# A third place for S5 tiles that come back from DRAM, and index gathers that stand behind the memory attention

## The chip, the core and the metric

The kernel runs on one core of a Trainium2 chip. The time is that of the device for one execution, in microseconds (us); of several executions the median is given. The profile is one execution, taken by the hardware profiler. The engines are called PE (matrix multiplication), PEld (its weight loads, which run beside it), DVE (VectorE), ACT (ScalarE), POOL (GpSimd) and SP (SyncE, which here only issues transfers).

## What is computed

One inference step of a small decoder with two layers, for a prompt of 1024 tokens and for 8 samples of 8 tokens that share the weights. Layer 0 mixes with a diagonal state-space model (S5), gates its output (GLU), and adds an attention over 256 memory tokens; layer 1 attends to a shared K/V cache with "forget" weights. This is the part that the change is about, cut from the reference:

```
# layer 0
z     = rmsnorm(h) @ w_in                              # 768 columns for S5, 256 for the memory queries
y_mem = softmax(q_mem k_mem^T / 8) v_mem               # 4 heads of 64, 256 memory tokens
y     = S5(z)                                          # scan over 48 groups of 64 states
g     = gelu(y);  y_main = g * sigmoid(g @ w_glu + b_glu)
h     = h + concat(y_main, y_mem) @ w_out              # then the MLP
# layer 1, samples only: the cached part of the forget sums
logf_past = cache_logf[page_table]                     # 8 samples x 2048 rows x 12 heads
f_past    = cumsum(logf_past)                          # used as a bias on the attention scores
```

## The kernel before, in words

Activations lie transposed: 1088 columns (1024 prompt tokens, 64 sample tokens) in four chunks `CH` of 272, features on the partitions. Every matrix product is made of three matmuls on rounded halves (`mm3`: high x high, high x low, low x high), so each operand is first split into a high and a low half: `split` has ACT write the high half (L221) and DVE, or POOL where it is told to, the low one (L222). A scheduler sets the order of instructions on each engine when the kernel is built; `after(x)` tells it that what is issued inside comes behind instruction `x`. Engines run their own rows strictly in that order, and wait for each other where data or a place in memory asks for it.

The stage around the change is called "glu". It does the following.

- The six weight tiles of `w_glu` are loaded and split; the second halves of three of them on POOL.
- The S5 output, six tiles of 128 features for all columns, had been written to DRAM (`yscr`) and is read back, re-arranged, into places `zs` of `zring` (L1280). Each tile is split into all four chunks of `yx`.
- For each of the four chunks, six output tiles `m` of the GLU: 18 matmuls each, tanh on ACT (L1324), two operations on DVE (L1325, L1326).
- After each of these 24 steps the generator `mem_attn` moves on by one unit. A unit is 128 prompt tokens and two heads: three matmuls 128x512 for the scores, a maximum (L791, DVE), two exponentials (L795, ACT), reciprocals (L796), two scalings (L798: the first on DVE, the second on POOL), four transposes on PE (L801), a copy out of PSUM (L803 ACT or L805 DVE), eight matmuls 64x128 in all for the output of a pair, and a store to `ymscr` for every second unit (L814). There are sixteen units. From the third block of tokens on, the attention of the samples moves on with them; its K and V tiles go through eight places `kvr`, cut from `extra`.
- `past_rows` (L1290 on): one index computation on POOL (L1291) and sixteen gathers, issued by POOL (L1293), that fetch cached log-forget rows by page into `fp`, which is `wf[2:4]`. `past_sums` (L1297 on): two scans on DVE over them (L1299), a copy (L1301), two subtractions (L1303), two stores to `fpast` (L1304). The sums are read only in layer 1.
- `out_proj` (L325 on) multiplies by `w_out`. Its eight raw weight tiles go through the places `wf` in turn; tiles 2 and 3, and 6 and 7, use the two places that `fp` uses. All of its loads are issued by SP, as are the stores to `fpast`.

`past_rows` is issued in the program before chunk 2, `past_sums` before chunk 3.

```
    zring = ga.sub(0, 2176).ring(2, 1088)
    extra = ga.words(4096)
```

`sub` names a part of `ga` and takes nothing from it, `words` takes; so `zring` and `extra` lie over each other, and a place of `kvr` that overlaps a place of `zring` can be loaded only when the S5 tile there has been split.

Of the kernel before, what the change touches and what calls it, by code (L numbers as in the profile page):

```python
# [12 lines left out]
ALU = mybir.AluOpType  # L13
# [35 lines left out]
def yoco_step(ctx: ExitStack, tc: tile.TileContext, I, O, upto=99, dbg=None):  # L49
    nc = tc.nc  # L50
    V, S, G, PE, SY = nc.vector, nc.scalar, nc.gpsimd, nc.tensor, nc.sync
# [251 lines left out]
    def after(ins):  # L303
        return tc.issue_after(ins.ins) if ins else nullcontext()
# [381 lines left out]
    def make_ev_qmem(l, first, ring):  # L686
# [3 lines left out]
            SY.dma_start(out=qmscr[l][:, i - first, CH[c][0]:CH[c][0] + w], in_=t)  # L690
        return ev

    def mem_attn(l, pf, pr, mb, oring, ys_to=None, extra=None):

        kb0, qr0, qf0, pw0 = pr.words(2048), pr.words(1024), pf.words(512), pf.words(3072)
# [84 lines left out]
        for b in range(8):  # L780
            qf = qfr([128, 2, 128])
            SY.dma_start(out=qf, in_=qmscr[l][:, :, 128 * b:128 * b + 128])
            qh = [qr([128, 2, 128], F32R) for _ in range(2)]
            split(qh[0], qh[1], qf)
            o = oring([128, 2, 128])
            for a in range(2):
                ps = mb([128, 2, 256])
                mm3(ps.rearrange("p e m -> p (e m)"), qh[0][:, a], qh[1][:, a], kb[0][:, a], kb[1][:, a],
                    True, True)
                st = stats([128, 12])  # L790
                V.tensor_reduce(st[:, 0:2], ps, axis=AX.X, op=ALU.max, negate=True)  # L791
                pw = prr([128, 2, 4, 128])
                p = pw[:, 0].rearrange("p (e t) m -> p e (t m)", e=2)
                for e in range(2):
                    S.activation(p[:, e], ps[:, e], AF.Exp, bias=st[:, e:e + 1], accum_out=st[:, 2 + e:3 + e])  # L795
                V.reciprocal(st[:, 4:6], st[:, 2:4])  # L796
                for e in range(2):
                    (G if e else V).tensor_scalar(p[:, e], p[:, e], st[:, 4 + e:5 + e], 0.0, op0=ALU.mult, op1=ALU.add)  # L798
                tp = mb([128, 4, 128])
                for i in range(4):  # L800
                    PE.transpose(tp[:, i, :], pw[:, 0, i, :], ident)  # L801
                if a:
                    S.activation(pw[:, 1], tp, AF.Copy)  # L803
                else:
                    V.tensor_copy(pw[:, 1], tp)  # L805
                po = mb([128, 128])
                for m in range(2):
                    for e in range(2):
                        h = 2 * a + e
                        mm(po[64 * e:64 * e + 64, :], vt[:, m, 64 * h:64 * h + 64], pw[:, 1, 2 * e + m, :],  # L810
                           m == 0, m == 1)
                S.activation(o[:, a, :], po, AF.Copy)
                if a:
                    SY.dma_start(out=ymscr[l][:, :, 128 * b:128 * b + 128], in_=o)  # L814
                if extra and b > 1:
                    next(sm, None)
                yield
# [442 lines left out]
    V.tensor_scalar(bgl, bgl, 0.5, None, op0=ALU.mult)  # L1260
    pf, pr = phase("glu", 4096, 2048 + 1024 + 1536)
    ga = joined(setA)
    zring = ga.sub(0, 2176).ring(2, 1088)
    extra = ga.words(4096)
    raws = ga.words(6 * 768)
    gring = Ring([raws.sub(384 * i, 384) for i in range(12)])
    wr_ = joined(wr)
    gwp = [wr_.sub(768 * i, 768) for i in range(10)] + [pr.words(768) for _ in range(2)]
    yx = [pair(c) for c in range(NC)]
    gw, gi = [], None  # L1270
    for i in range(6):
        raw = raws.sub(768 * i, 768).at([128, 6, 128])
        SY.dma_start(out=raw, in_=I["w_glu"][i])
        H, L = (gwp[2 * i + j].at([128, 6, 128], F32R) for j in range(2))
        x = split(H, L, raw, (G, V)[i % 2])
        gi = x if i % 2 == 0 else gi
        gw.append((H, L))
    for q in range(6):
        zs = zring([128, 8, 136])
# [26 lines left out]
    mem = mem_attn(0, pf, pr, Banks([2, 3, 4, 5, 6]), rsr, yx[NC - 1], extra)  # L1306
    for c, (t0, w) in enumerate(CH):
        if c == 2:
            with after(gi):
                past_rows()  # L1310
        if c == 3:
            with after(vi):
                past_sums()
        xH, xL = yx[c]
        held = []
        for m in range(6):
            ps = dbank([128, 512])
            for k in range(6):
                mm3(ps[:, :w], gw[m][0][:, k, :], gw[m][1][:, k, :], xH[:, k, :], xL[:, k, :],
                    k == 0, k == 5)  # L1320
            t = nt([128, w])
            y = gring([128, w])

            S.activation(t, ps[:, :w], AF.Tanh, scale=0.5, bias=bgl[:, m:m + 1])  # L1324
            V.tensor_tensor(y, xH[:, m, :].bitcast(F32), xL[:, m, :].bitcast(F32), op=ALU.add)  # L1325
            vi = V.scalar_tensor_tensor(y, t, 1.0, y, op0=ALU.add, op1=ALU.mult)  # L1326
            held.append(y)
            next(mem, None)
        n = 34 if c < NC - 1 else 26
        for m in range(6):  # L1330
            src = held[m].rearrange("p (t j) -> p t j", t=8)
            yH, yL = xH[:, m, :], xL[:, m, :]
            split(yH[:, 0:8 * n].rearrange("p (j t) -> p t j", t=8),
                  yL[:, 0:8 * n].rearrange("p (j t) -> p t j", t=8), src[:, :, 0:n], half=True)
            if c == NC - 1:
                split(yH[:, SAM].rearrange("p (t n) -> p t n", t=8),
                      yL[:, SAM].rearrange("p (t n) -> p t n", t=8), src[:, :, 26:34], half=True)
# [603 lines left out]
```

## Time and profile before

| | us |
|---|---|
| median of three runs | 2726.58 |
| the runs | 2719.97, 2726.58, 2727.91 |
| profiled execution, its own time | 2729.51 |
| its span, first to last instruction | 2727.7 |
| PE busy | 2564.0 (94 % of the span) |
| DVE busy | 1959.2 (72 %) |
| ACT busy | 1256.6 (46 %) |
| POOL busy | 1213.1 (44 %) |

"Busy" counts an engine's own operations; waiting, and issuing a transfer from SP, does not count. A start time is counted from the first instruction. A row with "x16" has put sixteen operations together; a bracket such as [5.46 <-POOL glu L798] says that the engine stood idle for 5.46 us before the row and that line 798 on POOL released it. A profile shows one execution, whose time lies a little over the median.

### The profile page before, as it was taken

To read this page: it belongs to the slowest core of one execution; us is meant where nothing else is said; L and a number is where in the kernel's file an instruction comes from. 1 tells how busy PE (TensorE), PEld (TensorE's weight loads), DVE (VectorE), ACT (ScalarE), POOL (GpSimd) and SP (SyncE) were. 2 spreads that over 40 slices of the span, in tenths; PEclk is the share of its full clock that TensorE was granted. 3 is DMA by queue.
4 is the path that set the end of the run, shared out by engine and by line. 5 is a ranking of instruction groups with operands and counts; after the bars stand their busy time and mean duration, and the time that the engine had idled before them with its cause. 6 is when DMAs were issued, how large, how long until landed. Compare 5 with 4: busy or idle time off the path is not lost.

```text
span 2727.7 us, 54053 instructions
## 1 busy us (share of the span) xinstructions
PE 2564.0 (94%) x20369; PEld 2392.2 (88%) x20369; DVE 1959.2 (72%) x3406; ACT 1256.6 (46%) x2612; POOL 1213.1 (44%) x1119
## 2 busy tenths in 40 slices
PE   6888899999998999999999999999989999899998
PEld 5777779899998999999889867777989999899998
DVE  8898665988886777794323278886588788677776
ACT  5433444566663222244322367775366665322224
POOL 4576310323321799842310455651032222179984
PEclk8999899999999999999999999999999999999999
DMA  6445352266558567443476889986226656866741
GB/s 200 106 104 146 117 163 76 91 242 243 229 228 324 232 254 277 178 167 102 150 259 222 268 290 308 304 294 218 91 87 244 236 227 234 318 242 244 285 169 67
DMA packets 242283, 561.66 MB, mean 206 GB/s; under 512 B 54053, under 2 KB 129382, under 8 KB 224614
## 3 DMA queue, kind: packets, MB, share of 16 engines
q1 hardware_dynamic: 212646, 548.50, 56.7%
q10 hardware_dynamic: 28864, 8.92, 1.4%
q8 instruction: 161, 2.64, 0.4%
q0 software_dynamic: 512, 0.79, 0.1%
q14 instruction: 100, 0.82, 0.1%
HBM read 386.19 MB, written 171.93 MB: 205 GB/s over the span
## 4 chain that ended last, share of the span: by engine, by line
PE 41%; DVE 18%; POOL 10%; DMA 10%; issue 6%; ACT 4%; SPq 0%; POOLq 0%; ACTq 0%; DVEq 0%
PE banks L209 39%; DMA hops<-plain 5%; DVE rounded L222 5%; POOL plain L630 4%; DVE plain L222 4%; PE banks L1667 1%; POOL plain L416 1%; DMA rounded<-hmid 1%; DVE plain L578 1%; POOL plain L646 1%; ACT plain L221 1%; POOL plain L422 1%; DMA hcnv<-plain 1%; POOL plain L417 1%; DMA plain<-fpast 1%
## 5 line engine op out<-in xcount | busy, mean ns | idle before, releaser
L209 PE MATMUL banks<-rounded 128*128 128x272 f32 (+3 forms) x11168 | 1552.6, 295 | 72.8 <-ACT rounded L221 18.3
L209 PEld LDWEIGHTS banks<-rounded 128*128 128x128 f32 x11168 | 1456.7, 191 | 120.3 <-ACT rounded L221 21.1
L221 ACT ACTIVATE rounded<-plain 128x512 fp32r<-128x512 f32 (+5 forms) x573 | 379.8, 676 | 637.5 <-PE banks L209 449.3
L222 DVE TENSOR_TENSOR rounded<-plain,rounded 128x512 fp32r<-128x512 f32 (+4 forms) x518 | 502.8, 976 | 121.7 <-ACT rounded L221 120.3
L209 PE MATMUL banks<-mlp,rounded 128*128 128x272 f32 x3816 | 516.8, 290 | 12.2 <-DVE plain L627 4.8
L209 PEld LDWEIGHTS banks<-mlp,rounded 128*128 128x128 f32 x3816 | 493.8, 189 | 17.2 <-DVE plain L627 5.3
L416 POOL TENSOR_TENSOR plain<-plain 128x512 f32<-128x512 f32 x60 | 103.9, 1731 | 705.9 <-DVE rounded L222 705.9
L630 POOL TENSOR_TENSOR plain<-plain,flex 128x544 f32<-128x544 f32 x192 | 289.8, 1520 | 37.7 <-DVE plain L629 34.8
L222 DVE TENSOR_TENSOR plain<-plain 128x544 fp32r<-128x544 f32 x212 | 171.1, 820 | 69.9 <-ACT plain L221 69.1
L221 ACT ACTIVATE plain<-plain 128x544 fp32r<-128x544 f32 x212 | 136.7, 650 | 111.6 <-DMA hops<-plain 99.1
L629 DVE TENSOR_TENSOR plain<-banks,plain 128x544 f32<-128x544 f32 x192 | 137.9, 718 | 50.3 <-PE banks L209 46.8
L422 POOL TENSOR_TENSOR plain<-plain 128x512 f32<-128x512 f32 x60 | 98.3, 1639 | 63.0 <-DVE rounded L222 62.6
L209 PE MATMUL banks<-flexr,rounded 128*128 128x272 f32 x816 | 114.5, 290 | 4.0 <-DVE flexr L222 4.0
L209 PE MATMUL banks<-layer 128*32 128x256 f32 (+3 forms) x1152 | 111.9, 368 | 5.5 <-DVE layer L1770 1.7
L579 ACT ACTIVATE plain<-plain 128x544 f32<-128x544 f32 (+1 forms) x136 | 83.2, 613 | 66.0 <-DVE plain L578 65.5
L209 PEld LDWEIGHTS banks<-flexr,rounded 128*128 128x128 f32 x816 | 107.8, 191 | 4.4 <-DVE flexr L222 4.4
L222 POOL TENSOR_TENSOR rounded<-plain,rounded 64x512 fp32r<-64x512 f32 (+2 forms) x55 | 77.9, 1424 | 67.1 <-ACT rounded L221 61.9
L222 POOL TENSOR_TENSOR rounded<-flex,rounded 128x544 fp32r<-128x544 f32 (+7 forms) x100 | 65.9, 668 | 83.7 <-ACT rounded L221 71.0
L578 DVE TENSOR_TENSOR plain<-banks,plain 128x544 f32<-128x544 f32 (+1 forms) x136 | 90.5, 666 | 11.8 <-PE banks L209 11.2
L222 DVE TENSOR_TENSOR rounded<-banks,rounded 128x512 fp32r<-128x512 f32 (+2 forms) x136 | 86.0, 637 | 13.1 <-ACT rounded L221 11.3
L221 ACT ACTIVATE rounded<-banks 128x512 fp32r<-128x512 f32 (+2 forms) x136 | 75.1, 559 | 42.0 <-PE banks L1667 29.3
L418 POOL TENSOR_TENSOR plain<-plain 128x512 f32<-128x512 f32 x60 | 91.7, 1528 | 2.8
(365 smaller groups left out, 3227.0 us busy)
## 6 DMA issues: line engine op xcount, KB each, us to landing
hops<-plain SPq DMA_DIRECT2D x196, 544.0 KB
rounded<-hops SPq DMA_DIRECT2D x66, 1088.0 KB
plain<-in_cache_kT SPq DMA_DIRECT2D x128, 384.0 KB
layer<-in_cache_v SPq DMA_DIRECT2D x128, 384.0 KB
mlp<-hops SPq DMA_DIRECT2D x32, 1088.0 KB
plain<-in_w_up SPq DMA_DIRECT2D x32, 1024.0 KB
plain<-in_w_down SPq DMA_DIRECT2D x28, 1024.0 KB
plain<-in_xT SPq DMA_DIRECT2D x8, 1088.0 KB
```

What stands on the lines that cost most here:

```text
L209: PE.matmul(out, a, b, start=first, stop=last)
L221: S.activation(H, src, AF.Copy)
L222: return e.tensor_tensor(L, src, H.bitcast(F32), op=ALU.subtract)
L416: G.tensor_tensor(a22, a21, a22, op=ALU.add)
L417: G.tensor_tensor(a21, a11, a21, op=ALU.subtract)
L418: G.tensor_tensor(a11, a22, a11, op=ALU.subtract)
L422: G.tensor_tensor(a12, a12, a11, op=ALU.subtract)
L578: V.tensor_tensor(x, ps, u, op=ALU.add)
L579: S.activation(x, x, AF.Relu)
L629: V.tensor_tensor(h, ps, h, op=ALU.add)
L630: G.tensor_tensor(h, h, u, op=ALU.add)
L646: G.tensor_tensor(hc, hc, hr[:, m, :], op=ALU.add)
```

## The change

Two edits. `zring` becomes three places of 1088 words instead of two; with it, places 0 to 6 of the eight `kvr` places overlap it, 0 to 4 before. And `past_rows` is ordered behind another instruction: not the third POOL split of `w_glu` (`gi`), but the last scaling of the memory attention that has been issued at that point of the program, the twelfth on POOL. No instruction is added or removed; line numbers after it are 2 or 3 higher.

```diff
+    pool = []
...
                 for e in range(2):
-                    (G if e else V).tensor_scalar(p[:, e], p[:, e], st[:, 4 + e:5 + e], 0.0, op0=ALU.mult, op1=ALU.add)
+                    pool[:] = [(G if e else V).tensor_scalar(p[:, e], p[:, e], st[:, 4 + e:5 + e], 0.0,
+                                                             op0=ALU.mult, op1=ALU.add)]
...
-    zring = ga.sub(0, 2176).ring(2, 1088)
+    zring = ga.sub(0, 3264).ring(3, 1088)
     extra = ga.words(4096)
...
-    gw, gi = [], None
+    gw = []
...
-        x = split(H, L, raw, (G, V)[i % 2])
-        gi = x if i % 2 == 0 else gi
+        split(H, L, raw, (G, V)[i % 2])
...
         if c == 2:
-            with after(gi):
+            with after(pool[0]):
                 past_rows()
```

The order of instructions is set when the kernel is built, and the two kernels' orders can be laid side by side. In the rows below a name such as glu_2469 or plain is a piece of on-chip memory, and xN counts rows that are alike.

POOL, from the three splits of `w_glu` to the sixteen scalings of the memory attention (L798), before:

```order
L222 TENSOR_TENSOR rounded<-plain,rounded 128x768 x3
L1291 TENSOR_SCALAR plain<-plain 96x16
L1293 DMA plain<-in_logf_rows,plain 96x128 x5
L703 MEMSET glu_2470 128x2048
L721 MEMSET glu_2469 128x512
L1293 DMA plain<-in_logf_rows,plain 96x128 x11
L726 COPY glu_2469<-plain 64x8x8 x4
L798 TENSOR_SCALAR glu_2469<-glu_2469,plain 128x256 x16
```

The same stretch of POOL after (L798 is now L800, L1293 is L1295):

```order
L222 TENSOR_TENSOR rounded<-plain,rounded 128x768 x3
L705 MEMSET glu_2470 128x2048
L723 MEMSET glu_2469 128x512
L728 COPY glu_2469<-plain 64x8x8 x4
L800 TENSOR_SCALAR glu_2469<-glu_2469,plain 128x256 x12
L1293 TENSOR_SCALAR plain<-plain 96x16
L1295 DMA plain<-in_logf_rows,plain 96x128 x16
L800 TENSOR_SCALAR glu_2469<-glu_2469,plain 128x256 x4
```

The index computation and all sixteen gathers moved behind twelve scalings; four scalings stand behind them.

PE at the end of the memory attention, from behind the transposes (L801) of the twelfth unit on; rows "rounded" of 272 columns are matmuls of the output projection, "glu" ones those of the attention; before:

```order
L209 MATMUL banks<-glu_2470 128x512 x3
L209 MATMUL banks<-glu_2469 64x128 x4
L209 MATMUL banks<-glu_2470 128x512 x3
L801 MATMUL banks<-plain,glu_2469 128x128 x8
L209 MATMUL banks<-glu_2469 64x128 x4
L209 MATMUL banks<-glu_2470 128x512 x3
L209 MATMUL banks<-glu_2469 64x128 x4
L209 MATMUL banks<-glu_2470 128x512 x3
L209 MATMUL banks<-rounded 128x272 x18
L801 MATMUL banks<-plain,glu_2469 128x128 x8
L209 MATMUL banks<-glu_2469 64x128 x8
L209 MATMUL banks<-rounded 128x272 x126
```

After, from the transposes of the thirteenth and fourteenth unit (the first row) on:

```order
L804 MATMUL banks<-plain,glu_2469 128x128 x8
L209 MATMUL banks<-glu_2469 64x128 x4
L209 MATMUL banks<-glu_2470 128x512 x3
L209 MATMUL banks<-glu_2469 64x128 x4
L209 MATMUL banks<-glu_2470 128x512 x3
L209 MATMUL banks<-rounded 128x272 x18
L804 MATMUL banks<-plain,glu_2469 128x128 x8
L209 MATMUL banks<-rounded 128x272 x2
L209 MATMUL banks<-glu_2469 64x128 x4
L209 MATMUL banks<-rounded 128x272 x23
L209 MATMUL banks<-glu_2469 64x128 x4
L209 MATMUL banks<-rounded 128x272 x149
```

In both, the row that follows is `rounded,mlp` x4, the first of the MLP. Ahead of the fifteenth and sixteenth unit's transposes nothing changed here; behind them 174 projection matmuls stand where 126 stood, and the third of them is the first that reads the second half of `w_out` tile 2. Projection matmuls that stood between earlier units are now behind.

DVE, around the two scans over the gathered rows (L1299) before:

```order
L805 COPY glu_2469<-banks 128x512
L1326 SCALAR_TENSOR_TENSOR plain<-flex_69,plain 128x272
L219 SCALAR_TENSOR_TENSOR rounded<-plain,rounded 128x8x34 x5
L1326 SCALAR_TENSOR_TENSOR plain<-flex_69,plain 128x272
L1299 SCALAR_TENSOR_TENSOR plain<-plain 96x1024
L219 SCALAR_TENSOR_TENSOR rounded<-plain,rounded 128x8x34
L1299 SCALAR_TENSOR_TENSOR plain<-plain 96x1024
L754 COPY glu_2469<-banks 128x256
L791 TENSOR_REDUCE plain<-banks 128x2
L1301 COPY plain<-plain 96x1
```

After (L1299 is L1301, L1301 is L1303, L1303 is L1305, L798 is L800, L805 is L808):

```order
L793 TENSOR_REDUCE plain<-banks 128x2 x2
L798 RECIPROCAL plain<-plain 128x2
L800 TENSOR_SCALAR glu_2469<-glu_2469,plain 128x256
L798 RECIPROCAL plain<-plain 128x2
L800 TENSOR_SCALAR glu_2469<-glu_2469,plain 128x256
L1301 SCALAR_TENSOR_TENSOR plain<-plain 96x1024 x2
L808 COPY glu_2469<-banks 128x512
L1303 COPY plain<-plain 96x1
L1305 TENSOR_SCALAR plain<-plain 96x1024 x2
L793 TENSOR_REDUCE plain<-banks 128x2
```

The scans moved from the middle of the GLU to between the thirteenth and fourteenth unit's scalings and the copy of their transposes. On SP the stores to `fpast` moved with them, and the loads of `w_out` tiles 2, 3, 6 and 7 now stand behind these stores; tiles 4 and 5 are loaded earlier. Before, all six stood behind the stores.

## Rows read from the trace of the kernel before

**Rows 1.** Windows: length, busy PE, PEld, DVE, ACT, POOL, granted PE clock, DMA

```profile
315.00:355.00 40.00, 40.00 (x324) 36.07 (x322) 30.82 (x60) 23.34 (x59) 3.50 (x5) 0.96 0.25 73
410.00:500.00 90.00, 89.18 (x704) 88.50 (x702) 59.21 (x83) 37.33 (x61) 6.24 (x4) 1.00 0.21 76
```

**Rows 2.** Chain of waits: start, duration, engine or transfer, line

```profile
373.06 9.60 DMA plain<-in_xT
...
386.64 2.18 DMA ymscr<-flex
388.88 3.13 DMA flex<-ymscr
...
408.54 11.53 PE banks L209 x93
```

**Rows 3.** POOL's timeline: start, duration, line, operation, idle before and releaser

```profile
283.63 0.73 POOL L1291 TENSOR_SCALAR plain<-plain 96x16 int32<-96x16 int32 x1 [11.88 <-DMA plain<-in_head_rows]
...
291.04 1.83 POOL L703 MEMSET glu<- 128x2048 f32 x1
...
293.50 0.93 POOL L1293 DMA_INDIRECT plain<-in_logf_rows,plain  x1 [0.16 <-issue]
...
297.31 2.47 POOL L1293 DMA_INDIRECT plain<-in_logf_rows,plain  x1 [0.30 <-issue]
300.08 0.92 POOL L1293 DMA_INDIRECT plain<-in_logf_rows,plain  x1 [0.30 <-issue]
...
310.25 0.92 POOL L1293 DMA_INDIRECT plain<-in_logf_rows,plain  x1 [0.30 <-issue]
...
312.78 0.95 POOL L726 COPY glu<-plain 64x64 f32<-64x64 f32 x3 [1.30 <-DMA plain<-in_logf_rows,plain]
313.83 0.93 POOL L798 TENSOR_SCALAR glu<-glu,plain 128x256 f32<-128x256 f32 x2
...
335.69 0.57 POOL L798 TENSOR_SCALAR glu<-glu,plain 128x256 f32<-128x256 f32 x1 [8.38 <-DVE plain L796]
...
389.33 0.57 POOL L798 TENSOR_SCALAR glu<-glu,plain 128x256 f32<-128x256 f32 x1 [2.68 <-DVE plain L796]
396.96 0.57 POOL L798 TENSOR_SCALAR glu<-glu,plain 128x256 f32<-128x256 f32 x1 [7.06 <-DVE plain L796]
```

**Rows 4.** PE's timeline at the gathers' end

```profile
314.36 0.69 PE L801 MATMUL banks<-plain,glu 128*128 128x128 f32 x2 [5.46 <-POOL glu L798]
```

**Rows 5.** ACT's timeline: the last two splits of S5 tiles, the first of w_out

```profile
280.50 1.39 ACT L221 ACTIVATE rounded<-plain 128x272 fp32r<-128x272 f32 x4 [3.96 <-DMA plain<-yscr]
283.04 1.39 ACT L221 ACTIVATE rounded<-plain 128x272 fp32r<-128x272 f32 x4 [1.15 <-DMA plain<-yscr]
...
362.35 1.06 ACT L221 ACTIVATE rounded<-plain 128x1024 fp32r<-128x1024 f32 x1 [2.86 <-DMA plain<-in_w_out]
```

**Rows 6.** Busy time in stretches of 4 us, columns as in rows 1

```profile
276.00:280.00 4.00, 1.73 (x6) 1.08 (x5) 4.00 (x13) 0.54 (x2) 0.00 (x0) 0.50 0.63 155
280.00:284.00 4.00, 2.23 (x8) 1.91 (x8) 2.69 (x9) 2.35 (x7) 0.37 (x1) 0.50 1.03 305
...
300.00:304.00 4.00, 4.00 (x32) 3.87 (x32) 4.00 (x13) 3.47 (x12) 3.31 (x3) 1.00 0.22 57
...
312.00:316.00 4.00, 1.64 (x8) 1.64 (x9) 0.69 (x1) 0.03 (x1) 1.81 (x5) 0.50 0.23 69
```

**Rows 7.** DVE's timeline: scan, subtractions, a unit's copy, a split of w_out

```profile
344.51 2.29 DVE L1299 TENSOR_TENSOR_SCAN plain<-plain 96x1024 f32<-96x1024 f32 x1
...
350.93 1.40 DVE L1303 TENSOR_SCALAR plain<-plain 96x1024 f32<-96x1024 f32 x2
...
357.64 0.68 DVE L805 COPY glu<-banks 128x512 f32<-128x512 f32 x1
...
363.44 1.23 DVE L222 TENSOR_TENSOR rounded<-plain,rounded 128x1024 fp32r<-128x1024 f32 x1 [3.37 <-ACT rounded L221]
```

**Rows 8.** Waits of 255 to 410 us: who waited for whom, us in total, times, longest

```profile
DVE plain L337 <- DMA plain<-in_xT: 3.3, 1, 3.3
```

## The prediction, made before the change was run

> **What bounds the kernel now.** I read the busy times by stretch first. TensorE (PE) is the bound over most of the program, 2564.0 of 2727.7 us on the page, so a change counts only where PE stands still, or where it makes PE stand still. All that the diff touches lies between 255 and 415 us. In 315 to 355 us PE is busy 40.00 of 40.00 us and from 410 on 89.18 of 90.00 [rows 1]: whatever has moved by 410 us is handed on to the end one for one, and nothing behind it can win it back or lose more.
>
> Then the chain of waits, for the places where PE is not the bound. Three concern the change. The last S5 tiles come back late: ScalarE (ACT) waits 3.96 and 1.15 us for them and starts the last split at 283.04 [rows 5], and VectorE (DVE), which makes the second halves, is busy 4.00 of 4.00 us in 276 to 280 and 2.69 of 4 in 280 to 284 [rows 6]. GpSimd (POOL) starts the sixteen gathers at 283.63 and ends the last at 310.25 + 0.92 = 311.17, and only then scales the first two units of the memory attention, at 313.83 [rows 3]; PE waits 5.46 us for that [rows 4], and its granted clock is 0.50 in 312 to 316 [rows 6]. Third, the row of 9.60 us for in_xT [rows 2]: those transfers share the memory with six w_out loads that are issued just ahead.
>
> **A third place for S5 tiles.** It adds no instruction. Of the six loads, those that had to wait for a place can start one tile earlier. Bounds: nothing, if DVE is what limits the splits (it is full until 280), and 3.96 + 1.15 = 5.1 us, if only the transfers do. DVE has 4 - 2.69 = 1.3 us to spare in 280 to 284, which the earlier tile can fill, and splits that move up take their time with them; I take **-3.0 us**, just above the middle. The price, two sample-V loads of early issue that now come behind the tiles, I put at nothing: the sample attention moves only with the fifth unit and later ones, whose scale was at 335.69 [rows 3], under PE's full stretch; if that cover failed it would be one lone load, about 3.1 us [rows 2].
>
> **Gathers away from the head.** POOL's scales of the first units no longer stand behind sixteen gathers. PE gets the 5.46 us back, and most of the ramp: at 0.50 for four microseconds half of the rate is lost, about 2 us. **-7.5 us**; from 5.5 if the low clock has another cause to 7.5. The scans on DVE (2.29 us each, [rows 7]) leave a stretch in which PE is full, so they give nothing there, at most 3 us. Also two of the six w_out loads now go early and four late, so part of the 3.3 us that DVE waits for in_xT [rows 8] may go: 0 to 3 us. I take nothing for these two, and use them for the range.
>
> **Gathers behind the twelfth scale.** The order shows that POOL now does twelve scales, the index arithmetic, sixteen gathers, four scales. The twelfth scale was at 389.33 [rows 3]. It moves by -3.0 - 7.5, and by another -2.4 because 18 fewer matmuls of the output projection stand ahead of it on PE (444 against 462, at 0.13 each): 376.4. Ends: 369 (5.1 at the front, 3.3 and about 2 more behind it) and 379.4 (nothing from the third place).
>
> What stands behind it: 0.57 for the scale itself, then index arithmetic and gathers. Measured, these took 311.17 - 283.63 = 27.5 us; two memsets in between, 291.04 to 293.50, took 2.3 of it, so 25.2 us. Most took 0.92 us with 0.30 to the next, 1.22 together; three took more than 2.2, up to 2.47 [rows 3]. At 1.22 throughout: 0.73 + 0.29 + 16 x 1.22 = 20.5 us. The three long ones lie in 297 to 307, and DVE was busy 4.00 of 4 us in 300 to 304, though a short one at 300.08 lies there too [rows 3, 6]. In the new place DVE has almost nothing to do, because it waits for the same gathers, so I take **21.5 us**, near the lower end.
>
> The Trainium skill has a rule for this: "SBUF — State Buffer", section "SBUF: two separate sides", says that a DVE operation in a two-port mode locks GpSimd out of their shared port, so that it cannot write descriptors for its own transfers. The trace agrees for the three long gathers and not for the one at 300.08. By the rule the block would be 20.5 us, as measured 25.2; a forecast by the one would be 1 us lower, by the other 3.7 us higher.
>
> Who waits for the block: the thirteenth and fourteenth scale stand behind it, and the transposes of these two units (the row of 8 between two groups of scores) need them. PE has only 14 instructions between the transposes of the units before and these, about 2 us. So PE, DVE and ACT stand still for nearly all of it; before, stretches of 18, 14, 16 and 18 projection matmuls stood among the last eight units. The block ends at 376.4 + 0.57 + 21.5 = 398.5.
>
> **What hangs on the gathers' end.** From there two paths run on. On PE: scales, transposes, copies and outputs of the last four units, about 13 us by the old times from 396.96 to 408.54. It is not the longer one. The other goes by memory: the gathered rows lie in places that the raw w_out tiles 2 and 3 need, and those two loads now stand behind the stores of the sums. Step by step: landing of the last gather 1.3 to 1.45 (POOL waits 1.30 for it [rows 3]); two scans 4.65; a copy of 0.68 that stands between; 0.14; one subtraction 0.70 [rows 7]; the store 2.18 (a 128 KB one alone [rows 2]) to 3.4, taken 2.8; the w_out load, 512 KB, 3.13 being the lone row of 272 KB [rows 2], taken 3.9; ACT's split 1.06 [rows 5] and DVE's 1.23 [rows 7]; and about 0.1 at each of eight hand-overs. **17.4 us**, ends 14.5 and 19.5. So the first matmul that needs the second half of w_out tile 2 starts at 398.5 + 17.4 = 415.9.
>
> To where before? Up to the first row in which PE's orders agree again (rounded,mlp), 172 rounded matmuls follow that one, the two ahead of it taken from 2 + 23 + 149. Before had 126 left when PE ran free at 408.54, at 11.53 / 93 = 0.124 us each [rows 2]. The same point was thus at 408.54 - 46 x 0.124 = 402.8. Loss: 415.9 - 402.8 = 13.1 us. PE was still before it, and the trace shows half rate after a stop (0.50 in 312 to 316 [rows 6]), so another 2 us. **+15 us.** The gains at the front are inside this: they only move the twelfth scale.
>
> Against the profiled execution: span 2727.7 + 15 = 2742.7, its time 2729.51 + 15 = 2744.5. That execution lies 2.9 us over the median of 2726.58, so the median goes to 2741.5.
>
> **Rivals.** A measurement of this kernel can tell about 0.3% from no change, 8.2 us.
>
> *The block is long again.* As measured before, 25.2 us, or more gathers of 2.4, with a tail of 19.5 and the twelfth scale at 378: 378 + 0.6 + 25.2 + 19.5 = 423.3, +20.5, and 3 us of low clock: 2750. For it: the long ones came in one stretch whose cause is not sure. Against: DVE is idle now.
>
> *The front gives all it can.* Twelfth scale at 369, block 20.5, tail 14.5: 404.6, +1.8 and 1 to 2 of clock: 2730, no difference. For it: the waits of 5.1 and 3.3 us are there to be had. Against: DVE is full until 280.
>
> *Faster.* The gathers' 0.92 us is not POOL's own work but a wait on a queue that was busy at the head; in a quiet place only the 0.30 of issue remains, a block of 1.0 + 16 x 0.3 = 5.8 us. With the twelfth scale at 371: 371 + 0.6 + 5.8 + 17.4 = 394.8, 8 us before 402.8, and no clock lost: 2718. It decides for faster once the block is under some 6 us. Against: the gathers took 0.92 at 300.08, beside full engines, as at 310.25, beside idle ones [rows 3].
>
> *The change does not do what it says:* no tile comes back earlier, since DVE holds the splits. The twelfth scale is at 379.4, and all behind it 3 us later: 2744.5. This lies inside the forecast.
>
> **How the numbers follow.** The forecast with its last variant, 2733 to 2748, has 0.62; the long block 0.17; the full front gain 0.15; the short block 0.06. The range leaves a tenth out on either side: 2729 to 2751. Faster by over 0.3% is the short block, 0.06. Within 0.3%, up to 2734.8, is the full front gain and the lowest part of the forecast, 0.17. Slower is the rest, 0.77.
>
> **What the new profile would show.** The first scales on POOL near 300 instead of 313.83, and no 5.46 us of PE behind them. The last S5 split about 280 instead of 283. Twelve scales, the last near 376; gathers until about 398, mostly of 0.92; in these 20 us PE nearly empty with a low clock. Then scans, store, w_out load in a row, and PE running free from about 416. I am wrong if the gathers land without PE waiting for the thirteenth scale, if w_out tile 2 is split long before PE wants it, or if the twelfth scale is reached before 370.

## The result, and the profile after

| | before | after |
|---|---|---|
| median of 22 runs each, us | 2724.63 | 2733.79 |
| lowest to highest | 2717.18 to 2729.97 | 2725.31 to 2739.09 |
| profiled execution, its own time | 2729.51 | 2735.09 |
| its span | 2727.7 | 2733.2 |

The ratio after to before is 1.0033, 95% interval 1.0026 to 1.0041: slower by 9.2 us, about as much as a measurement can tell from no change. Forecast were 2741.5 us, 2729 to 2751, and slower with 0.77.

The head of the stage improved as foreseen. PE's steady run starts at 281.60 (before 285.59), and POOL's first scales at 302.49 (before 313.83, [rows 3]). Then comes the block. POOL's timeline of the changed kernel: start, duration, line, operation, idle before and its releaser:

```profile
302.49 1.93 POOL L800 TENSOR_SCALAR glu<-glu,plain 128x256 f32<-128x256 f32 x2 [10.78 <-DVE plain L798]
...
371.93 0.57 POOL L800 TENSOR_SCALAR glu<-glu,plain 128x256 f32<-128x256 f32 x1 [0.41 <-DVE plain L798]
373.18 1.15 POOL L1295 DMA_INDIRECT plain<-in_logf_rows,plain  x1 [0.29 <-POOL plain L1293]
...
385.86 1.83 POOL L1295 DMA_INDIRECT plain<-in_logf_rows,plain  x1 [0.30 <-issue]
...
392.89 0.92 POOL L1295 DMA_INDIRECT plain<-in_logf_rows,plain  x1 [0.30 <-issue]
393.85 0.93 POOL L800 TENSOR_SCALAR glu<-glu,plain 128x256 f32<-128x256 f32 x2
```

From the end of the twelfth scale, 372.50, to the last gather's end, 393.81, are 21.3 us. PE's timeline there shows who pays:

```profile
394.39 1.13 PE L804 MATMUL banks<-plain,glu 128*128 128x128 f32 x4 [12.74 <-POOL glu L800]
...
407.06 0.52 PE L209 MATMUL banks<-rounded 128*128 128x272 f32 x2 [1.65 <-ACT rounded L221]
...
408.31 3.15 PE L209 MATMUL banks<-rounded 128*128 128x272 f32 x23
```

One wait of 12.74 us for the scale behind the gathers, and a last one of 1.65 us for the split of w_out tile 2. Ahead of the long wait PE still did 26 matmuls of the units before, until 381.65, so of the 21.3 us it stands still for about 15. The chain of waits names the way that ended last, by memory:

```profile
391.67 2.42 DMA plain<-in_logf_rows,plain
394.17 1.16 issue
395.43 2.35 DVE plain L1301
...
399.23 3.04 DMA fpast<-plain
402.29 3.55 DMA plain<-in_w_out
405.95 1.07 ACT rounded L221
407.04 1.24 DVE rounded L222
408.31 16.75 PE banks L209 x133
```

Windows of 4 us (length, busy time of PE, PEld, DVE, ACT, POOL, granted clock, share and rate of the DMA engines); to be laid beside [rows 1, 6]. A granted clock of 0.50 is the lower of two levels, 1.2 GHz, and 1.00 the upper, 2.4 GHz; a value between them is the mean of a stretch.

```profile
280.00:284.00 4.00, 2.97 (x12) 2.33 (x11) 4.00 (x12) 1.29 (x4) 0.00 (x0) 0.50 0.97 276
...
388.00:392.00 4.00, 0.00 (x0) 0.00 (x0) 0.00 (x0) 0.00 (x0) 3.08 (x4) 0.50 0.15 37
...
396.00:400.00 4.00, 3.73 (x20) 2.32 (x20) 3.96 (x6) 0.49 (x2) 0.00 (x0) 0.50 0.00 0
400.00:404.00 4.00, 4.00 (x21) 3.21 (x20) 1.76 (x6) 2.21 (x9) 0.57 (x1) 0.68 0.83 241
404.00:408.00 4.00, 2.35 (x23) 1.88 (x21) 1.31 (x2) 1.63 (x3) 0.64 (x1) 1.00 0.80 261
```

In 388 to 392 only POOL works. And DVE is full in 280 to 284 now: the third place moved the limit there from the transfers to DVE. ACT starts the last split of an S5 tile at 278.96, 4.1 us earlier than before.

**A ruler for the rest of the text.** POOL's additions at the head of the MLP (L416) come in the same order in every kernel. The first shows with what shift the stage is left, the fourth with what shift the head of the MLP is. From the POOL timelines, one profiled execution each, start in us and difference to before:

| kernel | first L416 | duration of the third | fourth L416 |
|---|---|---|---|
| before | 485.48 | 6.49 | 551.90 |
| after | +5.74 | 8.95 | +8.26 |

So 5.7 us come from the stage and 2.5 us more from one place in the MLP that the diff does not touch. The ruler has noise of its own: two kernels with the same order of rows, the changed one and add_on_dve below, leave the stage 3.0 us apart, early and early_add 2.3. A difference of 2 to 3 us between two rulers says nothing alone.

### The profile page after: what moved, and what is told of

It is laid out like the page before. It is cut to its first block, busy times and chain, and to the rows that moved or that the text cites. A ratio compares the mean times of both kernels' runs of the same rounds, so it can differ in the third digit from the quotient of the medians.

```text
span 2733.2 us, 54045 instructions
## 1 busy us (share of the span) xinstructions
PE 2561.8 (94%) x20369; PEld 2393.6 (88%) x20369; DVE 1958.0 (72%) x3406; ACT 1255.1 (46%) x2612; POOL 1208.5 (44%) x1119
## 3 DMA queue, kind: packets, MB, share of 16 engines
q10 hardware_dynamic: 28864, 8.92, 1.4%
## 4 chain that ended last, share of the span: by engine, by line
PE 43%; DVE 23%; DMA 11%; POOL 11%; issue 6%; ACT 4%; SPq 1%; POOLq 0%; ACTq 0%; DVEq 0%
PE banks L209 41%; DVE rounded L222 6%; DMA hops<-plain 5%; POOL plain L630 4%; DVE plain L222 4%; POOL plain L416 1%; PE banks L1669 1%; DMA rounded<-hmid 1%; POOL plain L646 1%; ACT plain L221 1%; DVE plain L578 1%; POOL plain L422 1%; ACT rounded L221 1%; DMA hcnv<-plain 1%; POOL plain L417 1%
## 5 line engine op out<-in xcount | busy, mean ns | idle before, releaser
L222 DVE TENSOR_TENSOR rounded<-plain,rounded 128x512 fp32r<-128x512 f32 (+5 forms) x518 | 502.3, 974 | 126.9 <-ACT rounded L221 124.5
L416 POOL TENSOR_TENSOR plain<-plain 128x512 f32<-128x512 f32 x60 | 106.7, 1779 | 714.7 <-DVE rounded L222 714.7
L422 POOL TENSOR_TENSOR plain<-plain 128x512 f32<-128x512 f32 x60 | 98.4, 1640 | 64.1 <-DVE rounded L222 63.6
L209 PE MATMUL banks<-rounded,layer 128*128 128x256 f32 x480 | 89.8, 299 | 2.7 <-ACT rounded L221 2.5
```

What stands on the lines that cost most here:

```text
L209: PE.matmul(out, a, b, start=first, stop=last)
L222: return e.tensor_tensor(L, src, H.bitcast(F32), op=ALU.subtract)
L416: G.tensor_tensor(a22, a21, a22, op=ALU.add)
L422: G.tensor_tensor(a12, a12, a11, op=ALU.subtract)
```

## The experiments

Twelve kernels. Medians are given with that of the kernel before on the same chip; "ruler" is the shift of the first and of the fourth L416 against before, with the third's duration between.

**ring3_only: the third place alone.**

```diff
-    zring = ga.sub(0, 2176).ring(2, 1088)
+    zring = ga.sub(0, 3264).ring(3, 1088)
```

> The third place for S5 tiles alone; the gathers stay where they were before. Theory (the third place is worth what PE's start of the free run showed, 285.59 to 281.60, 4.0 us, and the gathers' stall of about 5.5 us of PE remains): 4 us under the kernel before, and POOL's first scale near 310. Rival (the gathers are what binds at the head, and both memsets now stand behind all sixteen of them, so the keys of the memory attention are split later): the first scale stays at 313 or later, PE waits 8 to 10 us there instead of 5.5, and the time is that of the kernel before, within 2 us.

2741.63 against 2726.44 us, ratio 1.0060 (1.0039 to 1.0081). Ruler +10.76, 8.96, +13.28. The theory fails, and the rival too: it said the time of the kernel before, and this is 15 us over it. POOL's timeline, then PE's:

```profile
305.66 1.83 POOL L703 MEMSET glu<- 128x2048 f32 x1
...
324.06 0.56 POOL L798 TENSOR_SCALAR glu<-glu,plain 128x256 f32<-128x256 f32 x1 [14.74 <-DVE plain L796]
```

```profile
300.77 3.54 PE L209 MATMUL banks<-rounded 128*128 128x272 f32 x14 [5.58 <-issue]
```

Before, the memset stood behind five gathers, at 291.04 [rows 3]; here the scheduler put it behind sixteen, and the first scale comes at 324.06 instead of 313.83. The tiles were back earlier (the last split on ACT at 280.36), and PE could not use it. How much of this the memset explains is not shown. PE, DVE and ACT all but stood still from 295.0 to 300.8, ahead of the memset (0.22, 0.47 and 0.69 us busy), and PE was busy for 4.75 us of the 10.4 that follow, at waits for which the trace names no releaser. What stopped them stays open.

**behind_only: the gathers behind the twelfth scale, two places as before** (the second hunk of the diff without the first).

> The gathers behind the twelfth scale alone; two places for S5 tiles as before. Theory (block of 21.3 us and a tail of 14.5 us behind the twelfth scale, gains at the head lie inside it): the twelfth scale comes 4 us later than with both edits, at 376, PE runs free from about 412, and the time is 9 to 13 us over the kernel before, 3 to 4 us over the changed one. Rival (the third place gives the loss, by what it moves among the sample loads): no slower than before.

2737.60 against 2726.44, 1.0041 (1.0023 to 1.0058). Ruler +7.92, 8.93, +11.36. POOL's timeline:

```profile
298.73 0.81 POOL L800 TENSOR_SCALAR glu<-glu,plain 128x256 f32<-128x256 f32 x1 [9.37 <-DVE plain L798]
...
374.05 0.57 POOL L800 TENSOR_SCALAR glu<-glu,plain 128x256 f32<-128x256 f32 x1 [0.74 <-DVE plain L798]
```

The theory in its direction and in the block (PE waits 12.33 us for the scale), at half its size: 4 us were expected between the twelfth scales, and 2.1 were found. The stage ends 2.2 us later than with both edits, and the medians differ by about 2, but the two intervals overlap. So with the gathers out of the way the third place is worth about 2 us at most, not clear of noise; beside them the stage lost 10.8 by it. Alone both edits lose; together they lose less than the third place alone, and no more than the gathers' move alone.

**scales_on_dve: no scale behind the gathers.**

```diff
-                    pool[:] = [(G if e else V).tensor_scalar(p[:, e], p[:, e], st[:, 4 + e:5 + e], 0.0,
+                    pool[:] = [(G if e and (l or b < 6) else V).tensor_scalar(p[:, e], p[:, e], st[:, 4 + e:5 + e], 0.0,
```

> The changed kernel, but the last four units' second scale is on DVE instead of POOL, so no scale stands behind the gathers; the way by memory (gathered rows, scans, store, w_out tile 2) is untouched. Theory (the way by memory ends last, PE's own work on the last units is hidden under it): PE does the last four units while the gathers run, then stands still, and still runs free only near 408; the time is that of the changed kernel, within 3 us. Rival (POOL's block of the scales is the loss): PE never waits 12 us, and the time falls by 10 us or more against the changed kernel.

2730.52 against 2726.44, 1.0019 (1.0004 to 1.0034). Ruler +3.88, 6.49, +4.19. The chain below has the way by memory as the last to end, as the theory says, and the stage is left 1.9 us earlier than in the changed kernel, which is within the ruler's noise. By the times this kernel lies about 5 us under the changed one, between the theory's 3 and the rival's 10; 2.2 of it is the place in the MLP, where this kernel has the 6.49. But it is not a clean cut. PE did not get through the last units while the gathers ran; DVE and ACT stopped in the middle of them, at places whose releaser the trace doesn't name. Its chain of waits:

```profile
390.00 4.78 another core or an unknown queue
394.80 0.69 DVE plain L793
395.49 2.97 another core or an unknown queue
...
405.83 2.36 DVE plain L1301
408.40 0.76 DVE plain L1305
409.18 3.21 DMA fpast<-plain
412.40 5.45 DMA plain<-in_w_out
417.95 1.06 ACT rounded L221
419.06 30.95 PE banks L209 x243
```

**other_places: the gathered rows in the places of w_out tiles 0 and 1.**

```diff
-    fp = [x.at([96, 1024]) for x in wf[2:4]]
+    fp = [x.at([96, 1024]) for x in wf[0:2]]
```

> The changed kernel with the gathered rows in the places of w_out tiles 0 and 1 instead of 2 and 3: tiles 2 and 3 are loaded early and only tile 4 waits for the sums. The scales stay on POOL behind the gathers. Theory (two ways run out of the block, and PE's own work on the last four units, about 10 us behind the gathers' end, is nearly as long as the way by memory, 14.5 us): PE waits as long for the scales, about 12 us; 66 more projection matmuls (8 us) then stand behind the last units than in the changed kernel, so the time is 0 to 5 us over the changed kernel. Rival (the way by memory alone is the loss): 10 us or more under the changed kernel.

2745.61 against 2725.66, 1.0071 (1.0053 to 1.0089). Ruler +20.83, 6.49, +21.03. Worse than both expected. The block was the same (gathers 377.22 to 397.73), the second scan, store and load of a w_out tile still ran behind it to 414.12, and more projection matmuls stood behind that (240 behind the last units, 174 in the changed kernel). The cut took no step off the way, it only moved more work behind it.

**dve_other_places: both cuts.**

> As scales_on_dve, and the gathered rows lie in the places of w_out tiles 0 and 1 (and 4 and 5) instead of 2 and 3, so tile 2 is loaded without waiting for the sums and tile 4 waits, which PE needs about 18 us of projection later. Theory (both ways out of the block have to be cut): the last units run under the gathers, projection fills the rest, tile 4 is late by 0 to 5 us; 10 to 15 us under the changed kernel, 1 to 6 us under the kernel before. Rival (one of the two cuts was enough): the same time as the better of the two single cuts, within 3 us.

2762.33 against 2726.44, 1.0133 (1.0105 to 1.0162). Ruler +33.27, 8.93, +36.99. Neither the theory nor the rival. The scheduler put the second scan behind the last units (410.94 us) and the four w_out loads behind the stores (420.79), so PE's free run began at 425.43. With a scheduler between the source and the order, these two cuts did not separate the two ways out of the block, and no other run does: the next ones take the block away whole and so show what both ways cost together. Which of them ended last in the changed kernel is read from its own chain, and it was the last by 1.65 us only.

**spread: the gathers in four groups of four**, behind the 2nd, 4th, 6th and 7th scale.

```diff
-        if c == 2:
-            with after(pool[0]):
-                past_rows()
...
             next(mem, None)
+            if 6 * c + m in (1, 3, 5, 6):
+                at = 4 * (1, 3, 5, 6).index(6 * c + m)
+                with after(pool[0]):
+                    past_rows(range(at, at + 4))
```

> The changed kernel with the gathers in four groups of four, behind the 2nd, 4th, 6th and 7th scale, where POOL stood idle for 8 to 14 us each time; nothing is left out. A group is 4 x 1.22 = 4.9 us. Theory (what the change wins at the head is kept, and no block and no tail is left, since the rows have landed by 345): the twelfth scale near 372 and the last near 388; PE busy 40 of 40 us through the memory attention; 12 to 17 us under the kernel before. Rival (the gathers beside a busy DVE become long, 2.4 us each, and each group of 10 us stalls the next unit): no gain over the kernel before.

2722.10 against 2725.66, 0.9988 (0.9978 to 0.9999). Ruler -6.09, 8.95, -3.58. Under the kernel before by 3.6 us, about a quarter of what was expected, and the interval only just leaves out no change. The block is gone: the seventh scale is at 337.55, 16 us earlier than the 353.71 of before. Then the lead melts: the twelfth is at 381.51, 7.8 us ahead. First the way by memory, which now lies in the middle of the GLU (chain of waits):

```profile
343.81 2.57 DMA plain<-in_logf_rows,plain
346.50 2.35 DVE plain L1302
349.14 1.23 DVE rounded L222
351.33 0.67 DVE plain L1306
352.02 3.89 DMA fpast<-plain
355.98 4.79 DMA plain<-in_w_out
...
364.77 8.01 PE banks L209 x61
```

Then the last units, one behind the other with nothing of the projection between them; the granted clock fell to 0.73 in 385 to 410:

```profile
385.00:410.00 25.00, 21.52 (x132) 17.68 (x131) 9.75 (x20) 10.00 (x29) 2.26 (x4) 0.73 0.11 28
```

That clock does not belong to the order: spread_add below, with the same order up to here, has 0.93 in the same stretch.

**spread_other_places.**

> As spread, with the gathered rows in the places of w_out tiles 0 and 1. Theory: by 345 the sums are ready long before either pair of places is wanted, so this differs from spread by less than 3 us. Rival (the loads of w_out tiles 2 and 3 behind the sums' stores still hold PE): 3 us or more under spread.

2724.04 against 2725.66, 0.9988 (0.9977 to 0.9999): the same as spread. Ruler -7.19, 8.93, -4.79. With the rows landed at 347, it made no difference here whose places they use.

**plain_loads: no gathers on POOL.**

```diff
-        for i in range(16):
-            G.indirect_dma_start(...)
+        for i in range(2):
+            SY.dma_start(out=fp[i].rearrange("p (j k) -> p j k", j=8),
+                         in_=I["logf_rows"][768 * i:768 * i + 768].rearrange("(j p) k -> p j k", p=96))
```

> The changed kernel with the sixteen gathers replaced by two plain loads of as many rows from SP: it leaves out the lookup by page, so it reads other rows. POOL has no gathers at all. Theory: the price of the gathers in the changed kernel is the block and the tail, and spread hides all of it; this run is within 3 us of spread, 12 to 17 us under the kernel before. Rival (spread still pays for the gathers): 5 us or more under spread.

2721.91 against 2725.66, 0.9991 (0.9979 to 1.0002). Ruler -7.05, 8.92, -3.71: within 1 us of spread. So the gathers cost spread nothing that these runs can tell, and they cost the changed kernel 5.74 + 7.05 = 12.8 us of the stage by these two profiles, and as much by the medians. The scheduler issued the two plain loads at 236.20 and 251.75, well ahead of the stage, so they do not stand in the gathers' new place either. What is left is not the gathers'; the chain of this kernel names it:

```profile
359.36 10.09 DMA plain<-in_xT
...
379.02 2.15 DMA ymscr<-flex
381.23 3.22 DMA flex<-ymscr
```

The transfers of in_xT stand behind w_out loads again, as before (9.60 us, [rows 2]), and then the last units wait for their own store and load.

**add_on_dve: one addition at the head of the MLP on DVE.**

```diff
-        G.tensor_tensor(a22, a21, a22, op=ALU.add)
+        (V if n == 2 else G).tensor_tensor(a22, a21, a22, op=ALU.add)
```

> The changed kernel, but one addition at the head of the MLP (L416, 128x512, the third set of weights) is on DVE instead of POOL. There it took 8.95 us on POOL in every kernel in which DVE had an unbroken row of work beside it, and 6.49 in those in which DVE stood still for 0.45 us; the shift against the kernel before grew by 2.5 us right there in the first kind, and by less than 0.5 in the second. The order up to the end of the memory attention is the same as in the changed kernel. Theory (that POOL step is where 2.5 us of the loss come from): PE's run behind it starts 2.5 us or more earlier against the stage's end, so 2 to 5 us under the changed kernel. Rival (the jump has another cause, and DVE, full there, only gets longer): the same time as the changed kernel, or above.

2733.86 against 2726.02, 1.0025 (1.0015 to 1.0035). From the second to the next common L416 the changed kernel takes 51.65 us (508.51 to 560.16), this one 49.93, the kernel before 49.13. So this one profile gets back 1.7 of 2.5 us there. Whether the time itself fell is not settled: the interval overlaps that of the changed kernel, and this profile left the stage at 494.23, 3 us later with the same order. What stands in the way of the rest, POOL's timeline shows: the next step of POOL is now the one that lasts.

```profile
533.44 7.03 POOL L422 TENSOR_TENSOR plain<-plain 128x512 f32<-128x512 f32 x1 [16.93 <-DVE rounded L222]
```

**spread_add: the same on top of spread.**

> As spread (gathers in four groups of four behind the 2nd, 4th, 6th and 7th scale), with the same addition on DVE. Theory: spread enters the MLP 6.1 us ahead of the kernel before and lost 2.5 of it at that step, so 2 to 5 us under spread, 5 to 9 us under the kernel before. Rival: the same as spread.

2722.37 against 2726.02, 0.9989 (0.9978 to 0.9999): the same as spread, the rival. The fourth L416 stands at 548.98, 0.7 us later than in spread, and from the second to that one it takes 51.55 us for spread's 51.65. So here the same edit gives nothing, and the next step of POOL lasts again, 6.42 us. How much of the 2.5 us hangs on this one addition is left open by the two runs.

**early_add and early: gathers in groups of 6, 6 and 4 behind the 2nd, 4th and 6th scale, and the sums issued before chunk 2**; early_add with the addition on DVE, early without.

```diff
-        if c == 3:
+        if c == 2:
             with after(vi):
                 past_sums()
...
             next(mem, None)
+            js = {1: range(6), 3: range(6, 12), 5: range(12, 16)}.get(6 * c + m)
+            if js:
+                with after(pool[0]):
+                    past_rows(js)
```

> As spread_add, with the gathers in groups of 6, 6 and 4 behind the 2nd, 4th and 6th scale, and the sums issued one chunk earlier, so that the stores of the sums stand ahead of the sample loads and five w_out loads stand ahead of in_xT. Theory (in spread the way gathers, scans, stores, w_out still ran to 365 us, and holds the last units): rows landed by 335, sums stored by 342, 3 to 8 us under spread_add. Rival (the end of the stage is set by in_xT, ten us behind the w_out loads, and by the last units one after the other, as in plain_loads): within 3 us of spread_add.

2716.41 against 2726.02, 0.9971 (0.9959 to 0.9982); the stage is left 9.38 us before that of the kernel before.

> early_add with the addition back on POOL: gathers in groups of 6, 6 and 4 behind the 2nd, 4th and 6th scale, sums one chunk earlier, nothing else against the changed kernel. It tells whether early_add's gain over the kernel before (0.29%) is the gathers' place or the moved addition. Theory (the gathers' place; DVE's order here leaves the gap of 0.45 us in which that addition on POOL gets through): within 3 us of early_add, 5 to 9 us under the kernel before. Rival (the addition): 4 us or more over early_add.

2716.89 against 2724.94, 0.9973 (0.9961 to 0.9985). Ruler -7.06, 6.49, -7.07. It is the place of the gathers and of the sums, not the addition. This version, like early_add, beats both kernels: 8 us under before, and, by the two comparisons with it, 17 under the changed one. Two things differ from spread. The sums are stored from 343.5 instead of 352.0, so PE has w_out when it wants it (PE busy 28.82 of 30 us in 355 to 385, spread 25.69), and more projection matmuls stand among the last eight units. By the ruler that is worth 1.0 us at the end of the stage, within its noise. Most of the lead over spread, 3.5 us at the fourth L416, comes from the head of the MLP, where the scheduler's order here lets the addition through and the whole lead is kept:

```profile
515.76 6.49 POOL L416 TENSOR_TENSOR plain<-plain 128x512 f32<-128x512 f32 x1 [15.06 <-DVE rounded L222]
```

## Why the prediction was right, and where its numbers were off

The forecast was slower, by one block on POOL that PE waits out and a way by memory behind it. Both stand in the trace, the block with 21.3 us for the forecast 21.5. The size was +15; the stage gave +5.7, and 2.5 came from where none was expected. Of the 9.3 us by which the stage fell short, 4.5 are the twelfth scale, 0.2 the block, 2.9 what hangs on its end and 2 the low clock, 9.6 together. Term by term:

- **Third place, -3.0.** PE's run starts 4.0 us earlier; what the stage made of it is about 2 us at most (behind_only), not clear of noise. DVE became the limit, 4.00 of 4 in 280 to 284, as weighed.
- **Gathers away from the head, -7.5.** PE's wait of 5.46 us is gone (PE is busy 18.60 of 20.00 us in 296 to 316). The size can't be read from the first scale, which came 11.3 us earlier than before: in behind_only, without the third place, it came earlier still, at 298.73, 15.1 us before that of the kernel before. At the twelfth scale the gathers' move and the new order gave 15.3 us there (389.33 to 374.05), where this term and the 2.4 for the fewer matmuls add up to 9.9.
- **The twelfth scale, forecast 376.4, was at 371.93.** The first mis-sized term, by 4.5 us. The third place is not where they come from: without it the working gives 379.4, and behind_only measured 374.05, 5.4 us earlier; the third place then added 2.1 instead of 3.0. The 5.4 fit what was taken at nothing and kept for the range: three of the in_xT loads, issued at 372.46 behind six w_out loads before, go out at 352.70 behind two (in behind_only two of them at 353.49), and DVE's wait of 3.3 us [rows 8] is gone. No run separates the in_xT loads from the rest of the order.
- **What hangs on the gathers' end, forecast 17.4, was 14.5** (393.81 to 408.31). The step that failed: two scans of 4.65 us. They do not both wait for the last gather; the first eight fill the first half, and the first scan ran inside the block, so that one scan of 2.35 us hangs on the last gather. DVE's timeline of the changed kernel:

```profile
384.67 2.29 DVE L1301 TENSOR_TENSOR_SCAN plain<-plain 96x1024 f32<-96x1024 f32 x1 [3.57 <-DMA plain<-in_logf_rows,plain]
395.43 2.35 DVE L1301 TENSOR_TENSOR_SCAN plain<-plain 96x1024 f32<-96x1024 f32 x1 [8.47 <-DMA plain<-in_logf_rows,plain]
```

  Store and load were 3.04 and 3.55 for 2.8 and 3.9. PE's own way was, as said, the shorter one, but by 1.65 us only.
- **Half rate after the stop, +2.** In this profile it was 0: the clock was at 0.50 in 396 to 400, while PE did the last units, and at 1.00 from 404, before the free run at 408.31. It is not 0 in every execution: in add_on_dve, with the same order, the clock was 0.76 in 408 to 412 and 0.82 in 412 to 416, which on 3.32 and 4.00 us of busy PE is about 1.5 us.
- **The point before, 402.8.** 408.31 - 402.8 = 5.5; the ruler says 5.74. The way of counting the same point in two orders held.
- **"Handed on to the end one for one."** This step failed too, by 2.5 us. At the head of the MLP the third L416 on POOL, an addition of 1.3 us elsewhere, takes 6.49 us before and 8.95 after. First before, then after, the POOL row, and below each the DVE row in which they differ:

```profile
522.83 6.49 POOL L416 TENSOR_TENSOR plain<-plain 128x512 f32<-128x512 f32 x1 [15.06 <-DVE rounded L222]
```

```profile
528.61 1.86 DVE L222 TENSOR_TENSOR flexr<-plain,flexr 128x1088 fp32r<-128x1088 f32 x1 [0.45 <-ACT flexr L221]
```

```profile
528.57 8.95 POOL L416 TENSOR_TENSOR plain<-plain 128x512 f32<-128x512 f32 x1 [15.07 <-DVE rounded L222]
```

```profile
533.21 1.29 DVE L222 TENSOR_TENSOR flexr<-plain,flexr 128x1088 fp32r<-128x1088 f32 x1
```

  Before, DVE stood still for 0.45 us in front of this split, because ACT's half of it was late, and POOL's addition ended at 529.32. After, the scheduler had moved ACT's and DVE's rows there by a few places, DVE ran without a gap to 536.4, and the addition ended at 537.52. Apart from the kernel before, ten keep that addition on POOL, the changed one among them: the three with 6.49 (scales_on_dve, other_places, early) have the gap and pass on their shift within 0.4 us; the seven with 8.9 have none and lose 2.4 to 3.7 us. So the 2.5 us go with the gap in all eleven. That the gap is their cause is argued from this and not shown: no run changes the gap alone, and moving the addition gave 1.7 us in add_on_dve and 0.1 in spread_add.

The single profiles differ by 5.5 us of span, the medians by 9.2. The shift was +9.0 at 785 us and +6.2 at 2371; the profile of after got about 3 us back late, which the medians do not show. One profile can't tell more.

The weighed rule of the Trainium skill ("SBUF — State Buffer", "SBUF: two separate sides") was that a DVE operation in a two-port mode locks GpSimd out of their shared port, so that it can't write descriptors. The trace does not show which mode an operation is in, so what it can say is only whether long gathers lie beside a busy DVE, and they do. In the block DVE had little to do, fifteen gathers took 0.92 to 1.15 us, and the only long one (385.86, 1.83) lies on the scan at 384.67. In early_add two gathers ran beside a full DVE and were longer still; POOL's timeline and the window:

```profile
318.35 3.44 POOL L1296 DMA_INDIRECT plain<-in_logf_rows,plain  x1 [0.30 <-issue]
322.09 5.22 POOL L1296 DMA_INDIRECT plain<-in_logf_rows,plain  x1 [0.30 <-issue]
```

```profile
318.30:327.50 9.20, 8.43 (x74) 6.76 (x73) 9.14 (x17) 3.80 (x9) 8.66 (x2) 1.00 0.25 64
```

The prediction took the three long gathers before for agreement with the rule, and that says more than the trace does: the DVE rows beside the one at 297.31 take two sources or reduce (L1325, L219, L791), and nothing shows that they use that mode. The short gather at 300.08 beside a full DVE [rows 3, 6] stays unexplained; which DVE operations lock and which don't was not tried.

Of the rivals, the long block did not come, and the short block neither: no gather took less than 0.92 us, in any kernel or place. "The front gives all it can" came nearest: its tail of 14.5 was measured, and its twelfth scale of 369 lies 3 us under the 371.93, though it forecast no difference. The range held the time because those two ends were in it. That the time came out slower by more than 0.3% owes something to luck: it is so by 0.03%, and 2.5 of the 9.2 us arose in a place for which the prediction had nothing; the stage's 5.7 alone would be 0.2%.

## What to carry to other kernels

A row of gathers on GpSimd is work of that engine, 1.22 us each here; put behind one unit of a pipeline, it stops all that stand behind it, so lay it in small groups into the engine's own idle time, early enough that what it feeds has landed before it is wanted. An order read from the built kernel gives the direction of such a loss; the size here hung on loads and scans that moved along with it. Two edits that shift the same stage must be timed together and apart: here each alone lost 11 to 15 us and both together 9, though the 11 and the 9 are not clear of each other. And where a scheduler sets the order, compare the orders in the stages behind the edit as well, above all where GpSimd works beside a full VectorE.

## What the runs showed of the hardware that was not expected

An addition on GpSimd that takes 1.3 us elsewhere took 8.95 us beside an unbroken row of VectorE work and ended about 1.1 us after it; in the four kernels where VectorE paused for 0.45 us in that row it took 6.49. The kernels whose VectorE did not pause there were the ones that lost 2.4 to 3.7 us at that place, so an engine that was late went with a faster stage. No run changes the pause alone.
